# Sixteen of 43 contraction tiles of the down projection as 2x2 block products with seven multiplications

## The chip, the cores and the metric

The kernel runs on one core of a Trainium2 chip. A core has a tensor engine for matrix products (PE, with PEld its loads of the stationary operand), a vector engine (DVE), a scalar engine (ACT), GpSimd (POOL), and SyncE (SP), which here issues nearly all DMAs. Each engine takes its instructions in the order in which they stand in the program and waits at each until its operands are there. The metric is the device time of one execution in microseconds (us).

## The reference

The program is one decoder layer over 256 tokens of width 2048, all in float32: a norm, a mix of three branches with an output projection `w_o`, a second norm, a gated MLP, a final norm. The part that matters here is the end of it:

```python
h = rms_norm(x, norm2_g[l])
up = causal_dwconv(h @ ffn_up[l], ffn_conv_w[l])          # 2048 -> 2 x 5504
gt, vl = jnp.split(up, 2, axis=-1)
x = x + (jax.nn.silu(gt) * vl) @ ffn_down[l]              # 5504 -> 2048
...
return rms_norm(x, final_g)
```

The last product has 256 rows (tokens), a contraction of 5504 = 43 tiles of 128, and 2048 columns.

## The kernel before, in words

A float32 product is made of three passes in the type float32r: an operand is cut into an upper part and a lower rest, and the sum is hi\*hi + lo\*hi + hi\*lo. So each weight tile that arrives by DMA in a `raw` buffer (128x1024, 512 KB, 5 buffers) is **split**: ACT writes the upper part `wh` (line 75), DVE the rest `wl` (line 76). `wh` and `wl` have three buffers each, so that a split may run three chunks ahead of the products that use it.

**The up projection** (`gemm_t`) runs over 43 groups of 256 columns, four chunks each. Behind each group stands `up_group`: it folds the PSUM result, applies the three convolution taps and the gate, and splits the result into one tile of `fa` (lines 181 and 182). `fa` holds 43 tiles, [128 channels, upper parts of 256 tokens | rests of 256 tokens].

**The down projection** (`gemm_n`, called at lines 589 to 593) runs over four blocks of 512 columns. A chunk is two contraction tiles of 512 columns; it is split once, and then gives 2 tiles x 2 token halves x 3 passes = 12 matmuls of 128x512, eight with `wh` (lines 143 and 145) and then four with `wl` (line 150). Each block has a pair of PSUM banks of its own out of three, so the result of one block is taken up (`take`: the residual sum on DVE, its square sum on ACT, the product with the final gain) while the next one runs. `posts` is the list of such pieces of work; they are emitted behind the second chunk of the next block. For the last block the first 128 tokens are finished before the others, and `finish` scales and stores each half.

A scheduler sets the order of the instructions on each engine when the program is built, from the order in which they are emitted and its own estimate of times; `background` is a list of small pieces that `tick` emits one by one behind the newest split. The first chunks of the down projection are loaded by `first_weights` before the last `up_group` is emitted (line 555). The final pool `fin` is opened behind that.

Of the kernel before, what the change touches and what calls it, by code (L numbers as in the profile page):

```python
# [12 lines left out]
F32 = mybir.dt.float32  # L13
F32R = mybir.dt.float32r
# [16 lines left out]
# Columns of the packed per-channel parameters: [128, NV], a channel tile per column.  # L31
# [11 lines left out]
def hybrid_block(ctx: ExitStack, tc, xT, x, vec, w_in, pool_w, pool_p, conf_p, sconv_p, w_o, up, down, fg, out):  # L43
    """The activations lie transposed (channels on partitions, tokens free) up to w_o and from there
    to ffn_down. A float32 product is three passes of float32r: an operand a = ah + al exactly, ah
    its upper and al its lower 12 bits of mantissa, and the sum is ah*bh + al*bh + ah*bl."""
# [20 lines left out]
    def load_w(src, dst=None):  # L67
        """[128, kt, n] of a weight -> its upper and lower parts."""
# [59 lines left out]
    def gemm_n(src, act, nk, kt=2, ahead=(), last=None, finish=None):  # L128
# [3 lines left out]
        if last is None:  # L132
            ps = psg.tile([P, 2, 512], F32, name="g")
            out = [ps[:, t, :] for t in range(2)]
        else:
            out = [psm.tile([P, 512], F32, name="m") for t in range(2)]

        def products(ts, k0, wh, wl):
            n = wh.shape[1]
            for kk in range(n):  # L140
                k = k0 + kk
                for t in ts:
# [4 lines left out]
            for kk in range(n):  # L147
                k = k0 + kk
                for t in ts:
# [3 lines left out]
        nb = nk - (8 if last is not None else 0)  # L153
        for i, k0 in enumerate(range(0, nb, kt)):
            n = min(kt, nb - k0)
            products((0, 1), k0, *(ahead[i] if i < len(ahead) else load_w(src[:, k0:k0 + n, :])))
            if i == 1:
                run_posts()
        if last is not None:
            chunks = [(k0, load_w(src[:, k0:k0 + 2, :], [last[:, o + k0 - nb:o + k0 - nb + 2, :] for o in (0, 8)]))  # L160
                      for k0 in range(nb, nk, 2)]
            for t in range(2):
                for k0, w in chunks:
                    products((t,), k0, *w)
                finish(t, out[t])
# [474 lines left out]
```

## Time and profile before

| | us |
|---|---|
| median of three runs | 1506.58 (1506.28 to 1507.52) |
| span of the profiled execution, first to last instruction | 1504.9 |
| PE busy | 1488.4 (99% of the span) |
| DVE busy | 1079.8 (72%) |
| ACT busy | 765.7 (51%) |
| share of PE in the chain that ended last | 97% |

The run's time is 1.7 us longer than the span: that lies around the first and the last instruction. In the profile, matmuls are pipelined: the recorded 0.39 us of one 128x512 matmul is longer than the step from one to the next, so the step is read from rows that hold several. The views used below are the page, the chain of waits in order of time, groups of instructions by line and shape, the timeline of single engines, busy times by stretch with the granted clock, and the DMA issues.

### The profile page before, as it was taken

How to read it: one execution, taken by the hardware profiler on the slowest of the kernel's cores; microseconds unless marked ns; L12 is line 12 of the kernel's file. 1: busy time of each engine (PE TensorE's matmuls, PEld its weight loads, DVE VectorE, ACT ScalarE, POOL GpSimd, SP SyncE). 2: the span in 40 equal slices, each digit the busy share in tenths (PEclk: the TensorE clock that was granted, in tenths of full speed). 3: DMA queues.
4: the chain of work that ended last, by engine and by line, in shares of the span. 5: the costliest groups of instructions: out<-in, count | busy, mean ns of one | idle time of the engine just before them, and what ended most of it. 6: DMA issues, size and time to landing. Idle time of an engine off the chain costs nothing.

```text
span 1504.9 us, 21171 instructions
## 1 busy us (share of the span) xinstructions
PE 1488.4 (99%) x8090; PEld 1291.8 (86%) x8090; DVE 1079.8 (72%) x1450; ACT 765.7 (51%) x1019; POOL 23.8 (2%) x87
## 2 busy tenths in 40 slices
PE   7999999999999999999999999999999999999997
PEld 6888888888888888888888888888888888888886
DVE  5878888888888786666557777777777777455453
ACT  6544454454445565554555555555555555344343
POOL 0000000000000200000000000000000000000000
PEclk9999999999999999999999999999999999999999
DMA  8755555565555555557655555555555556666663
GB/s 276 242 190 186 181 181 191 190 199 189 193 186 188 188 183 188 190 186 248 183 181 190 188 190 186 191 188 187 189 188 190 189 188 212 197 197 195 189 196 119
DMA packets 81446, 290.08 MB, mean 193 GB/s; under 512 B 9152, under 2 KB 9664, under 8 KB 80960
## 3 DMA queue, kind: packets, MB, share of 16 engines
q1 hardware_dynamic: 80912, 287.94, 58.7%
q8 instruction: 63, 1.03, 0.3%
q10 hardware_dynamic: 432, 0.79, 0.1%
q14 instruction: 39, 0.32, 0.1%
HBM read 286.60 MB, written 2.10 MB: 192 GB/s over the span
## 4 chain that ended last, share of the span: by engine, by line
PE 97%; DMA 2%; issue 0%; ACT 0%; DVE 0%; DVEq 0%; POOLq 0%; POOL 0%; ACTq 0%
PE g L114 50%; PE g L118 26%; PE g L143 6%; PE g L150 6%; PE g L145 6%; PE m L150 1%; PE m L143 1%; PE m L145 1%; DMA raw<-in_w_in 1%; DMA raw<-in_x 0%; DMA raw<-in_xT 0%; PE m L510 0%; DMA g<-in_vec 0%; ACT wh L75 0%; DVE hT L251 0%
## 5 line engine op out<-in xcount | busy, mean ns | idle before, releaser
L76 DVE TENSOR_TENSOR wl<-raw,wh 128x1024 fp32r<-128x1024 f32 (+1 forms) x537 | 649.6, 1210 | 365.8 <-ACT wh L75 360.8
L75 ACT CAST wh<-raw 128x1024 fp32r<-128x1024 f32 (+1 forms) x537 | 556.1, 1036 | 634.6 <-PE g L114 238.3
L114 PE MATMUL g<-hT,wh 128*128 128x512 f32 x2912 | 733.9, 394 | 7.8 <-DVE hT L251 4.3
L114 PEld LDWEIGHTS g<-hT,wh 128*128 128x128 f32 x2912 | 524.7, 189 | 102.4 <-ACT wh L75 8.8
L118 PEld LDWEIGHTS g<-hT,wl 128*128 128x128 f32 x2912 | 399.1, 191 | 29.4
L118 PE MATMUL g<-hT,wl 128*128 128x256 f32 x2912 | 407.7, 283 | 0.0
L281 DVE SCALAR_TENSOR_TENSOR confwork<-confwork,vecs 128x256 f32<-128x256 f32 x240 | 107.8, 477 | 0.0
L145 PE MATMUL g<-wh,fa 128*128 128x512 f32 x258 | 100.4, 389 | 0.0
L143 PE MATMUL g<-wh,fa 128*128 128x512 f32 x258 | 100.4, 389 | 0.0
L546 DVE SCALAR_TENSOR_TENSOR cv<-sp,vecs,cv 128x256 f32<-128x256 f32 x172 | 71.7, 479 | 0.0
L150 PE MATMUL g<-wl,fa 128*128 128x512 f32 x258 | 69.2, 389 | 0.0
L171 ACT COPY fold_b<-g 128x512 f32<-128x512 f32 x115 | 66.9, 581 | 0.0
L145 PEld LDWEIGHTS g<-wh,fa 128*128 128x128 f32 x258 | 48.4, 188 | 10.1
L150 PEld LDWEIGHTS g<-wl,fa 128*128 128x128 f32 x258 | 48.4, 188 | 10.1
L143 PEld LDWEIGHTS g<-wh,fa 128*128 128x128 f32 x258 | 48.4, 188 | 10.0
L143 PE MATMUL g<-wh,merged 128*128 128x512 f32 x128 | 50.1, 391 | 0.0
L145 PE MATMUL g<-wh,merged 128*128 128x512 f32 x128 | 49.8, 389 | 0.0
L181 ACT CAST fa<-cv 128x256 fp32r<-128x256 f32 x43 | 17.5, 407 | 55.0 <-DVE cv L549 55.0
L174 DVE TENSOR_TENSOR fold_o<-g,fold_b 128x512 f32<-128x512 f32 x60 | 41.0, 683 | 0.0
L544 ACT ACTIVATE cv<-sp,vecs 128x256 f32<-128x256 f32 x86 | 39.0, 501 | 0.1
L150 PE MATMUL g<-wl,merged 128*128 128x512 f32 x128 | 34.2, 389 | 0.0
L182 DVE TENSOR_TENSOR fa<-cv,fa 128x256 fp32r<-128x256 f32 x43 | 18.3, 425 | 19.8 <-ACT fa L181 19.8
(131 smaller groups left out, 891.0 us busy)
## 6 DMA issues: line engine op xcount, KB each, us to landing
raw<-in_w_in SPq DMA_DIRECT2D x188, 512.0 KB, 3.6
raw<-in_up SPq DMA_DIRECT2D x172, 512.0 KB, 4.7
raw<-in_down SPq DMA_DIRECT2D x84, 512.0 KB, 3.8
raw<-in_w_o SPq DMA_DIRECT2D x32, 512.0 KB, 3.4
raw<-in_pool_p SPq DMA_DIRECT2D x16, 512.0 KB, 3.7
raw<-in_sconv_p SPq DMA_DIRECT2D x16, 512.0 KB, 4.8
raw<-in_conf_p SPq DMA_DIRECT2D x16, 512.0 KB, 3.6
raw<-in_x SPq DMA_DIRECT2D x4, 512.0 KB, 6.6
```

Source lines behind the costliest of these rows:

```text
L75: nc.scalar.copy(dst[0], raw)
L76: held["split"] = nc.vector.tensor_sub(dst[1], raw, dst[0].bitcast(F32)).ins
L114: nc.tensor.matmul(ps[:, j, :], lhsT=wh[:, kk, j * P:(j + 1) * P], rhs=act[:, k0 + kk, :], start=(k0 + kk == 0), stop=False)
L118: nc.tensor.matmul(ps[:, j, 0:S], lhsT=wl[:, kk, j * P:(j + 1) * P], rhs=act[:, k0 + kk, 0:S], start=False, stop=(k0 + kk == nk - 1))
L143: nc.tensor.matmul(out[t], lhsT=act[:, k, t * P:(t + 1) * P], rhs=wh[:, kk, :], start=(k == 0), stop=False)
L145: nc.tensor.matmul(out[t], lhsT=act[:, k, S + t * P:S + (t + 1) * P], rhs=wh[:, kk, :], start=False, stop=False)
L150: nc.tensor.matmul(out[t], lhsT=act[:, k, t * P:(t + 1) * P], rhs=wl[:, kk, :], start=False, stop=(k == nk - 1))
L171: nc.scalar.copy(b, ps[:, :, S:2 * S])
L174: nc.vector.tensor_add(out, ps[:, :, 0:S], b)
L281: nc.vector.scalar_tensor_tensor(acc[:, c, :], src, w, acc[:, c, :], op0=ALU.mult, op1=ALU.add)
L544: nc.scalar.activation(cv[:, h, :], sp[:, h, 0:S], AF.Copy, scale=V("ffn_w", c))
L546: nc.vector.scalar_tensor_tensor(cv[:, h, :], sp[:, h, q:q + S], V("ffn_w", c + q), cv[:, h, :], op0=ALU.mult, op1=ALU.add)
```

## The change

The contraction tiles 0 to 15 are taken in eight pairs (k, k+1). With the two token halves as rows, A is a 2x2 block matrix (a11, a21 from tile k, a12, a22 from tile k+1), and the weight's two tiles with two blocks of 512 columns give B. Winograd's form of Strassen's scheme makes the product with seven block multiplications and sums of blocks on both sides. The other 27 tiles stay plain, four block products each. A block product is three matmuls of 128x512, as before.

- The columns now run in two chunks `c` of 1024 (`chunk_pair`), each with four banks for the results ("11", "12", "21", "22") and four for the products p1, p5, p6, p7 that are added into several results: all eight banks of PSUM, the same ones for both chunks.
- `block_sums` makes the left sums once, for two pairs at a time (four calls, emitted one behind each of the first four plain tiles): a sum of the two parts of `fa`, four sums or differences of 128x2x128, and the splits of the results. s3 takes the place of a21 in `fa`.
- `pair` makes the right sums t1 to t4 per pair and chunk on DVE, four operations of 128x512, and splits four pieces where two plain tiles have two.
- `spread_products` adds p1, p5, p6, p7 to the residual `x1` after the last pair of a chunk, six operations on DVE. `take` and `finish` are now called per token half at the end of each chunk, directly and not through `posts`.
- The order of chunk 0 is nine plain tiles, then eight times a pair and two plain tiles, then two plain tiles; of chunk 1 it is eight times a pair and three plain tiles, then three. The last three tiles of each chunk are done for the first token half and then for the second.
- `first_weights` is no longer called for the down projection.

The diff, cut:

```diff
+SP = {i: 2 * i for i in range(0, 8, 2)}
+NS = 2 * len(SP)
...
-        ahead = first_weights(down[0])
         run_posts()
...
+    def block_sums(i):
+        def go():
+            r = fin.tile([P, 1024], F32, name="t", bufs=3)
+            v = fa[:, SP[i]:SP[i] + 4, :]
+            r = r.rearrange("p (k s) -> p k s", k=4)
+            nc.vector.tensor_add(r, v[:, :, 0:S].bitcast(F32), v[:, :, S:2 * S].bitcast(F32))
...
+            nc.vector.tensor_add(s1, a21, a22)
+            nc.vector.tensor_sub(s2, s1, a11)
+            nc.vector.tensor_sub(s4, a12, s2)
+            nc.vector.tensor_sub(s3, a11, a21)
+            o = sums[:, i:i + 2, :, :]
+            nc.scalar.copy(o[:, :, :, 0:P], q[:, :, 0:3, :])
+            nc.vector.tensor_sub(o[:, :, :, P:S], q[:, :, 0:3, :], o[:, :, :, 0:P].bitcast(F32))
+            d = v.rearrange("p (i e) s -> p i e s", e=2)[:, :, 0, :]
+            nc.scalar.copy(d[:, :, P:S], s3)
+            nc.vector.tensor_sub(d[:, :, S + P:2 * S], s3, d[:, :, P:S].bitcast(F32))
...
+    def product(name, left, right, first, last):
+
+        (ah, al), (bh, bl) = left, right
+        nc.tensor.matmul(bank[name], lhsT=ah, rhs=bh, start=first, stop=False)
+        nc.tensor.matmul(bank[name], lhsT=al, rhs=bh, start=False, stop=False)
+        nc.tensor.matmul(bank[name], lhsT=ah, rhs=bl, start=False, stop=last)
...
+            w11, = split_n(b11, 512)
+            nc.vector.tensor_sub(t1, b12, b11)
+            nc.vector.tensor_sub(t3, b22, b12)
+            put("p1", left_tile(k, 0), w11, last)
+            w1, w3 = split_n(t13, 1024)
+            nc.vector.tensor_sub(t2, b22, t1)
+            nc.vector.tensor_sub(t4, b21, t2)
+            put("p5", left_sum(i, 0), w1, last)
+            put("p7", left_tile(k, 1), w3, last)
+            w2, w4 = split_n(t24, 1024)
+            put("p6", left_sum(i, 1), w2, last)
+            w21, w22 = split_n(o, 1024)
+            put("21", left_tile(k + 1, 1), w4)
+            put("11", left_tile(k + 1, 0), w21)
+            put("12", left_sum(i, 2), w22)
...
+        for t in range(2):
+            for j, (k, _) in enumerate(tail):
+                plain(k, (t,), w[j], j == 2)
+            close(t)
...
             for t in range(2):
+                nc.vector.tensor_add(xs[:, t], bank["p1"].unsqueeze(1).broadcast_to([P, 2, 512]), xs[:, t])
+            nc.vector.tensor_add(xs[:, 0, 1], bank["p6"], xs[:, 0, 1])
+            for p in ("p6", "p7"):
+                nc.vector.tensor_add(xs[:, 1], bank[p].unsqueeze(1).broadcast_to([P, 2, 512]), xs[:, 1])
+            nc.vector.tensor_add(xs[:, :, 1], bank["p5"].unsqueeze(1).broadcast_to([P, 2, 512]), xs[:, :, 1])
...
+    def take(t):
+
+        for n in range(2):
+            residual(bank[f"{t + 1}{n + 1}"], x1[:, t, 512 * n:512 * n + 512], ss3[:, t, n:n + 1])
+        nc.vector.tensor_mul(x1[:, t, 0:1024], x1[:, t, 0:1024], fgb[:, 0:1024])
...
+    chunk_pair(0, first, take)
+    chunk_pair(1, second, finish)
```

How the change moves instructions is seen in their order on an engine. First DVE at the seam from the up to the down projection. Before, behind the last `up_group` (its last product of the gate, line 549, and its split into `fa`, line 182) there are only splits of down weights, one per chunk:

```order
L76 TENSOR_TENSOR wl_11859<-raw_11856,wh_11858 128x1024
L549 TENSOR_TENSOR cv_11776<-cv_11776 128x256
L182 TENSOR_TENSOR fa_7180<-cv_11776,fa_7180 128x256
L76 TENSOR_TENSOR wl_11877<-raw_11874,wh_11876 128x1024
L76 TENSOR_TENSOR wl_11895<-raw_11892,wh_11894 128x1024
L76 TENSOR_TENSOR wl_11913<-raw_11910,wh_11912 128x1024
```

Now the four `block_sums` stand there (line 562 the sum r, 567 to 570 the four sums, 573 and 576 the splits). From the first r to the split of the eighth plain tile, `wl_11962`, which may be called S7 (the tiles of chunk 0 counted from S0), there are 30 DVE instructions: 4 of r, 20 of 128x2x128, 3 of 128x6x128, and the splits of S5, S6 and S7. The last twelve rows of the stretch:

```order
L562 TENSOR_TENSOR t_11894<-fa_7180 128x1024
L569 TENSOR_TENSOR t_11867<-t_11865,t_11867 128x2x128
L576 TENSOR_TENSOR fa_7180<-t_11867,fa_7180 128x2x128
L567 TENSOR_TENSOR t_11896<-t_11894 128x2x128
L570 TENSOR_TENSOR t_11896<-t_11894 128x2x128
L573 TENSOR_TENSOR hT_11783<-t_11867,hT_11783 128x6x128
L568 TENSOR_TENSOR t_11896<-t_11896,t_11894 128x2x128
L576 TENSOR_TENSOR fa_7180<-t_11896,fa_7180 128x2x128
L569 TENSOR_TENSOR t_11896<-t_11894,t_11896 128x2x128
L586 TENSOR_TENSOR wl_11962<-raw_11959,wh_11961 128x1024
L573 TENSOR_TENSOR hT_11783<-t_11896,hT_11783 128x6x128
L586 TENSOR_TENSOR wl_11980<-raw_11977,wh_11979 128x1024
```

The splits of S7 and of S8 (`wl_11980`) have moved behind all 20 of these small operations. On PE, at S7, six matmuls with upper parts (`wh_11961` of S7 and `wh_12001` of the first pair's p1) stand ahead of the first one that needs `wl_11962`:

```order
L596 MATMUL g_11784<-wh_11961,fa_7180 128x512
L597 MATMUL g_11784<-wh_11961,fa_7180 128x512
L596 MATMUL g_11785<-wh_11961,fa_7180 128x512
L597 MATMUL g_11785<-wh_11961,fa_7180 128x512
L596 MATMUL m_11787<-wh_12001,fa_7180 128x512
L597 MATMUL m_11787<-wh_12001,fa_7180 128x512
L598 MATMUL g_11784<-wl_11962,fa_7180 128x512
```

Before, no matmul of a later chunk stood ahead of a chunk's own: a chunk was eight with `wh` and four with `wl`.

The second place is DVE where one block of columns ends and the next begins. Before, the taking up of block 0 (lines 496 and 570) stood behind two splits of block 1's weights:

```order
L76 TENSOR_TENSOR wl_12178<-raw_12175,wh_12177 128x1024
L76 TENSOR_TENSOR wl_12196<-raw_12193,wh_12195 128x1024
L496 TENSOR_TENSOR x1_6534<-g_11795,x1_6534 128x512 x2
L76 TENSOR_TENSOR wl_12219<-raw_12216,wh_12218 128x1024
L570 TENSOR_TENSOR x1_6534<-x1_6534,fgb_11793 128x2x512
L76 TENSOR_TENSOR wl_12237<-raw_12234,wh_12236 128x1024
```

Now, between chunk 0 and chunk 1 (lines 483 and 680 are `take`; g_11784 holds banks 11 and 12, g_11785 banks 21 and 22; 630, 631, 634, 635 make t1, t3, t2, t4; `t_12816` is the t1 of the pair after; `wl_12727` is the split of t1 and t3 for p5 and p7, `wl_12739` that of t2 and t4 for p6 and 21):

```order
L483 TENSOR_TENSOR x1_6534<-g_11784,x1_6534 128x512 x2
L631 TENSOR_TENSOR t_12715<-raw_12713,raw_12711 128x512
L483 TENSOR_TENSOR x1_6534<-g_11785,x1_6534 128x512
L680 TENSOR_TENSOR x1_6534<-x1_6534,fgb_11781 128x1024
L483 TENSOR_TENSOR x1_6534<-g_11785,x1_6534 128x512
L586 TENSOR_TENSOR wl_12727<-t_12715,wh_12726 128x1024
L680 TENSOR_TENSOR x1_6534<-x1_6534,fgb_11781 128x1024
L634 TENSOR_TENSOR t_12716<-raw_12713,t_12715 128x512
L630 TENSOR_TENSOR t_12816<-raw_12812 128x512
L635 TENSOR_TENSOR t_12716<-raw_12713,t_12716 128x512
L586 TENSOR_TENSOR wl_12739<-t_12716,wh_12738 128x1024
L586 TENSOR_TENSOR wl_12746<-raw_12713,wh_12745 128x1024
```

The adds of chunk 0's last banks and both products with the gain now stand ahead of the splits that chunk 1's first pair needs.

## Rows read from the trace of the kernel before

**Rows 1.** The page: span; busy time, share, instructions; granted clock by slice, in tenths.
```profile
span 1504.9 us, 21171 instructions
PE 1488.4 (99%) x8090; PEld 1291.8 (86%) x8090; DVE 1079.8 (72%) x1450; ACT 765.7 (51%) x1019; POOL 23.8 (2%) x87
PEclk9999999999999999999999999999999999999999
```
**Rows 2.** The chain that ended last, at the seam: start us, us, what.
```profile
1261.30 0.95 PE g L118 x8
1272.25 0.91 PE g L150 x4
1274.97 0.91 PE g L150 x4
```
**Rows 3.** Groups by shape, 1225 to 1505 us: busy us, mean ns; idle before, releasers.
```profile
L76 DVE TENSOR_TENSOR wl<-raw,wh 128x1024 fp32r<-128x1024 f32 x91 | 111.4, 1225 | 109.4 <-ACT wh L75 109.4
L75 ACT CAST wh<-raw 128x1024 fp32r<-128x1024 f32 x91 | 95.8, 1053 | 129.6 <-PE g L145 92.9 <-PE m L145 20.4 <-issue 12.7
L496 DVE TENSOR_TENSOR x<-g,x 128x512 f32<-128x512 f32 x6 | 3.9, 686 | 0.0
L570 DVE TENSOR_TENSOR x<-x,fgb 128x1024 f32<-128x1024 f32 x3 | 3.7, 1217 | 0.0
L76 DVE TENSOR_TENSOR wl<-raw,wh 128x512 fp32r<-128x512 f32 x4 | 2.8, 692 | 4.4 <-PE g L150 4.1 <-issue 0.2
L182 DVE TENSOR_TENSOR fa<-cv,fa 128x256 fp32r<-128x256 f32 x5 | 2.1, 425 | 2.4 <-ACT fa L181 2.4
L181 ACT CAST fa<-cv 128x256 fp32r<-128x256 f32 x5 | 2.0, 407 | 6.5 <-DVE cv L549 6.5
```
**Rows 4.** DVE in order of time at the seam: start us, us, instruction [idle before].
```profile
1266.40 1.67 DVE L546 SCALAR_TENSOR_TENSOR cv<-sp,vecs,cv 128x256 f32<-128x256 f32 x4
1267.98 1.22 DVE L76 TENSOR_TENSOR wl<-raw,wh 128x1024 fp32r<-128x1024 f32 x1
1269.12 0.42 DVE L549 TENSOR_TENSOR cv<-cv 128x256 f32<-128x256 f32 x1
1270.01 0.42 DVE L182 TENSOR_TENSOR fa<-cv,fa 128x256 fp32r<-128x256 f32 x1 [0.47 <-ACT fa L181]
1273.42 1.23 DVE L76 TENSOR_TENSOR wl<-raw,wh 128x1024 fp32r<-128x1024 f32 x1 [1.23 <-ACT wh L75]
```
**Rows 5.** Stretches: PE, PEld, DVE, ACT, POOL busy (x instructions), PEclk, DMA, GB/s.
```profile
1300.00:1350.00 50.00, 50.00 (x222) 41.42 (x221) 24.94 (x22) 20.64 (x24) 0.00 (x0) 1.00 0.63 194
1497.00:1498.00 1.00, 0.00 (x0) 0.00 (x0) 0.21 (x1) 0.68 (x2) 0.00 (x0) 1.00 0.34 123
1498.00:1499.00 1.00, 0.00 (x0) 0.00 (x0) 0.41 (x1) 0.41 (x1) 0.55 (x1) 0.61 0.00 0
1499.00:1500.00 1.00, 0.00 (x0) 0.00 (x0) 0.87 (x2) 0.53 (x1) 0.00 (x0) 0.50 0.00 0
```
**Rows 6.** DMA issues, 1262 to 1496 us: KB each, median us to landing.
```profile
raw<-in_down SPq DMA_DIRECT2D x77, 512.0 KB, 4.1
```
**Rows 7.** The end, in order of time: start us, us, engine, instruction [idle before].
```profile
1495.58 0.61 PE L150 MATMUL m<-hT,fa 128*128 128x512 f32 x2
1496.23 0.69 DVE L496 TENSOR_TENSOR x<-m,x 128x512 f32<-128x512 f32 x1 [1.80 <-PE m L150]
1496.96 0.63 ACT L497 ACTIVATE scratch<-x 128x512 f32<-128x512 f32 x1 [2.87 <-DVE x L496]
1497.71 0.21 DVE L580 TENSOR_SCALAR r<-ss,part 128x1 f32<-128x1 f32 x1 [0.79 <-ACT scratch L497]
1498.59 0.62 DVE L584 TENSOR_SCALAR x<-x,r 128x768 f32<-128x768 f32 x1 [0.67 <-POOL r L581]
1499.13 0.75 DVE L586 SCALAR_TENSOR_TENSOR x<-x,r,fgb 128x512 f32<-128x512 f32 x1
1499.90 0.33 SPq L587 DMA_DIRECT2D out<-x  x1
```

More of the change, by code (lines that the diff above doesn't have):

```diff
@@ L148, in products @@
                 k = k0 + kk
-                for t in ts:
+                for t in range(2):
                     nc.tensor.matmul(out[t], lhsT=act[:, k, t * P:(t + 1) * P], rhs=wl[:, kk, :],
                                      start=False, stop=(k == nk - 1))
[L153 to L156, printed above, removed]
             if i == 1:
                 run_posts()
[L159 to L165, printed above, removed]
         return out
@@ new lines, in chunk_pair, with put, plain, pair @@
+    def chunk_pair(c, order, close):
+        seen = set()
+        live = {"11": 0, "12": 0, "21": 0, "22": 0}
+        pairs_left = [sum(1 for _, i in order if i >= 0)]
+        def put(name, left, right, last=False):
+            product(name, left, right, name not in seen, last)
+            seen.add(name)
+        def plain(k, ts, w, last=False):
+            for t in ts:
+                for n in range(2):
+                    put(f"{t + 1}{n + 1}", left_tile(k, t), w[n], last)
+        def pair(k, i):
+            e, o = (load_raw(down[c][:, k + j:k + j + 1, :])[0][:, 0, :] for j in range(2))
+            last = pairs_left[0] == 1
+            b11, b12 = halves(e)
+            b21, b22 = halves(o)
+            t13, t24 = (fin.tile([P, 1024], F32, name="t", bufs=3) for _ in range(2))
+            (t1, t3), (t2, t4) = halves(t13), halves(t24)
+            w11, = split_n(b11, 512)
[13 more added lines that the diff above has]
+            put("12", left_sum(i, 2), w22)
+            pairs_left[0] -= 1
+            if last:
+                posts.append(spread_products(c))
+        tail = order[-3:]
+        for k, i in order[:-3]:
+            if i >= 0:
+                pair(k, i)
+            else:
+                plain(k, (0, 1), split_n(load_raw(down[c][:, k:k + 1, :])[0][:, 0, :], 1024))
+                run_posts()
+                tick(1)
+        assert all(i < 0 for _, i in tail)
+        w = [split_n(load_raw(down[c][:, k:k + 1, :])[0][:, 0, :], 1024) for k, _ in tail]
+        for t in range(2):
+            for j, (k, _) in enumerate(tail):
+                plain(k, (t,), w[j], j == 2)
+            close(t)
@@ L589, in hybrid_block @@
-    for n in range(3):
-        posts.append(take(n, gemm_n(down[n], fa, KF, ahead=ahead)))
-        ahead = ()
-    room = hp.tile([P, 16, 512], F32R, name="hT")
-    gemm_n(down[3], fa, KF, last=room, finish=finish)
+        nc.scalar.activation(x1[:, t, 0:1024], x1[:, t, 0:1024], AF.Copy, scale=r)
+        nc.scalar.dma_start(ov[:, t, 0:1024], x1[:, t, 0:1024])
+        for n in range(2):
+            o = 1024 + 512 * n
+            nc.vector.scalar_tensor_tensor(x1[:, t, o:o + 512], x1[:, t, o:o + 512], r, fgb[:, o:o + 512], op0=ALU.mult, op1=ALU.mult)
+            nc.sync.dma_start(ov[:, t, o:o + 512], x1[:, t, o:o + 512])
@@ new lines, in hybrid_block @@
+    single = [(k, -1) for k in range(KF) if not any(p <= k < p + 4 for p in SP.values())]
+    paired = [(SP[i] + 2 * j, i + j) for i in SP for j in range(2)]
+    for i in SP:
+        background.append(block_sums(i))
+    first, second = list(single[:9]), []
+    for n, p in enumerate(paired):
+        first += [p, *single[9 + 2 * n:11 + 2 * n]]
+        second += [p, *single[3 * n:3 * n + 3]]
+    first += single[9 + 2 * len(paired):]
+    second += single[3 * len(paired):]
+    chunk_pair(0, first, take)
```

62 lines of the change are left out of this document (36 added, 26 removed).

## Prediction, made before the changed kernel ran

> **What bounds the kernel now.** I read the page first: PE is busy 99% of the span [rows 1]. The chain of waits then tells whether busy is also necessary: from the last up matmuls on it holds nothing but PE, and two groups of four matmuls that close successive chunks start 2.72 us apart [rows 2]. So 12 matmuls of 128x512 cost 2.72 us, 0.227 us each, without a gap. The stretch in the middle of the down projection shows what lies beside that: DVE busy 24.9 of 50 us, ACT 20.6 [rows 5]. The groups by shape show that DVE's idle time ends on ACT's cast and ACT's on PE [rows 3]: weights are split as soon as PE frees a buffer, not when DVE finds time. Matmuls removed are time removed, as long as every split still comes before its matmul. That is the question, since the change puts its additions on DVE, which has half its time free on average but works in order. Hence I go through DVE's order at each place where much is added.
>
> DVE prices [rows 3]: 1.225 us for 128x1024, 0.69 for 128x512, 0.425 for 128x256, also with an operand in PSUM (0.686). Behind a 1.22 us split the next instruction starts after 1.14 [rows 4], so I count steps: 1.14, 0.61 and 0.34, or the full duration plus 0.04 where an operation needs the one just ahead of it. The 128x6x128 splits lie between rows 256 and 1024: 0.96 us, step 0.87. The 128x2x128 operations have no row of their own; I give them the step of 256 elements. No less is to be had; strided operands and waits could make it 0.46.
>
> **Removed.** Eight pairs in two chunks spare one block product each: 16 x 3 = 48 matmuls of 1032, 48 x 0.227 = **10.9 us**. Bytes loaded stay the same.
>
> **The seam, S0 to S8.** The last up matmuls end at 1261.30 + 0.95 = 1262.25 [rows 2]. `first_weights` is gone, but the scheduler put the first casts and loads ahead of the last `up_group` anyway, so nothing is lost there; the load of the final gain and the allocation of `fin` come behind the loads of S0 to S8. The split into `fa` ended at 1270.43 [rows 4]. A chunk's `wh` is now free after its 11th matmul instead of its 8th, 0.68 us later, so I put this at 1271.2. From there DVE has, to the end of S7's split: four r and the splits of S5, S6, S7, 7 x 1.14 = 8.0; 20 small ones, 20 x 0.34 = 6.8; three of 128x6x128, 2.6; and about 0.1 of waiting for ACT. Sum 17.5, so `wl_11962` is there at 1288.7. S5 (1273.6) and S6 (1278.6) come in time. PE reaches S7 at 1262.25 + 7 x 2.72 = 1281.3, has six matmuls that need no `wl_11962` (1.36), and stands still from 1282.7: **6.1 us** lost. With small operations at 0.46 it is 8.5; I keep 5.5 to 9.
>
> S8's split follows at 1290.7, just in time. Behind it DVE makes w11's split, t1 to t4 and the split for p5 and p7 in a row: 1.21 + 0.61 + 0.61 + 0.73 + 0.73 + 1.23 from there to 1295.0, while PE, through S8 at 1293.4, wants that split at 1294.1. With the p6 split 0.35 late too, the first pair loses **1.3 us** (0 to 2).
>
> **Steady pairs.** A pair and two plain tiles take PE 45 x 0.227 = 10.2 us; DVE 5 x 0.61 + 5 x 1.14 and some dependent steps, 9.0; ACT five casts at 1.05 and one of half the size, 5.9. It holds, but with little to spare at one point: the split for p6 stands behind t1 of the pair after, which waits for that pair's raw tile. This load is issued when a plain tile's split, 3.7 us before the pair starts, frees its buffer; at 4.1 us to landing [rows 6] t1 is done about 1.0 us into the pair, the split at 2.2, and PE wants it at 2.5. I cost it at nothing; should landing take a microsecond more, 0.7 us per pair, 5 us for seven. Chunk 1 has three plain tiles per pair and more room.
>
> **End of each chunk.** The six adds of `spread_products`, 5 x 1.14 + 0.61 = 6.3 us of DVE, stand among the splits of the last pair and of the tail. The first waits for the last p1 and delays the split behind it; the scheduler gave PE upper-part matmuls to fill in. Counting DVE from 0.9 us (p1 done and seen) over eight steps of 1.14 and 0.61, the first tail tile's split ends at 9.6, and PE, with 0.2 lost before, is at 8.6 when it needs it: **1.2 us**, in both chunks 2.4 (1 to 4).
>
> **Between the chunks.** Let E be the end of the last matmul's step in chunk 0. The adds of banks 11 and 12 occupy DVE until about E - 0.2, since PE's order finishes these banks only seven matmuls before E; then t3 (E + 0.4), the add of 21 (E + 1.05), the product with the gain (2.2), the add of 22 (2.8), and only then the split for p5 and p7, at E + 4.0. PE has done p1 and four upper-part matmuls and waits. Then come the second product with the gain (5.1), t2, the next t1, t4 (7.0), ACT's cast of t2 and t4 (8.1), DVE's split (9.4): PE finishes p6 at E + 9.65, where 12 matmuls without a wait would be at 2.72. **6.9 us** lost (5 to 9). Before, two splits stood ahead of this work and the next block had banks of its own; now PE has no work without these splits.
>
> **The end.** Before, the last add started 0.2 us after E and the last DMA was issued at E + 3.87 (E = 1495.58 + 2 x 0.227 = 1496.03) [rows 7]. Now the first token half's scaling, two of 0.75 us, fills DVE until E + 0.7, as its banks close only 18 matmuls (4.1 us) before E; then two adds (2.0), squares and their sums (2.75), one reduction more than before (0.25) and the 0.9 us from sums to scaling as in rows 7 (3.9), two scalings (5.3), the DMA. **1.45 us** more (0.5 to 2).
>
> **The clock.** With PE idle from 1496.2, the granted clock read 1.00 in 1497 to 1498, 0.61 in the next microsecond and 0.50, which is 1.2 GHz, from 1499 on [rows 5]. PE's waits of 6.1 us at S7 and 3.5 us ahead of p6 are idle stretches of that kind, so I expect the lower level behind them. No row here shows matmuls at 1.2 GHz. From nothing, if the clock returns at once, to about 2.7 us per chunk of 12 for as long as it stays: I take 0.3 us at the seam (the wait of the first pair absorbs most) and 1.7 at the boundary, **2.0 us** (0 to 8). The Trainium skill asks to leave no idle gaps between bursts of matmuls, or the array goes back to the slow clock (TensorE: Matmul & The Clock Gate, "Why this matters for your kernels"); the trace agrees as far as the fall goes, with 0.50 after the last matmul, and without that rule this term would be nothing and the sum below 7.25.
>
> **Sum.** -10.9 + 6.1 + 1.3 + 2.4 + 6.9 + 1.45 + 2.0 = +9.25 us: span 1504.9 + 9.25 = 1514.2, and with the 1.7 us that lie between span and median, **1516 us**. By the terms' ends, it is -10.9 + 5.5 + 0 + 1 + 5 + 0.5 + 0 = +1.1 to -10.9 + 9 + 2 + 5 + 4 + 9 + 2 + 8 = +28; not all go one way.
>
> **Rivals.**
> - *The sums are done in time.* The stall at S7 is the difference of two long walks; if DVE needs 11.4 us instead of 17.5 up to S7, PE does not wait there. For it: DVE is idle 25 of 50 us. Against: that idle time lies behind casts, and the stretch has 30 instructions, nearly all without a wait between. Then 1516 - 6.1 - 1.3 - 0.3 = 1508.3, not slower by the bound used here. Decided where S7's split ends before 1283. 0.13.
> - *The waits between the chunks overlap too*, as DVE's queue lets splits through that I place behind the adds: without either place, -10.9 + 2.4 + 1.45 = -7, 1499.5. The order of the program speaks against it, half a microsecond here or there is all I see. 0.07.
> - *The clock stays low.* If PE runs at half rate over the rest of S7, S8 and the first pair (41 matmuls, 9.3 us more, of which waits absorb 1.3) and half as long at the boundary, 1516 - 2 + 8 + 4 = 1526. For it: PE's busy share is low for 9 us at the boundary. Against: the clock stands at its highest digit in all 40 slices, the first with PE's early waits too [rows 1]. The rule named above would work this way too, as a mechanism of this kernel. 0.08.
> - *Loads bind in chunk 0's pairs*: 5 us, 1521. For it: the small room at the next raw tile; against: 4.1 us is a median under nearly the same load. 0.10.
>
> That leaves 0.62 for the forecast, itself spread over 1511 to 1521. What a measurement of this kernel tells from no change is 0.2%, 3 us: 1503.6 to 1509.6. Faster 0.08, the same 0.15 (the first rival and the low edge of the forecast), slower 0.77. Range 1507 to 1522: two in ten are left out, the second rival and the long clock.
>
> **What would show it.** PE's waits: one of about 6 us for DVE (line 598) near 1283 us, one or two of 1 us in the first pair and ahead of each tail, about 7 us in pieces in p5 to p6 of chunk 1's first pair, each ended by DVE's split (line 586) or ACT's cast behind it. PE's matmuls 48 fewer; granted clock below 1.00 behind the two long waits; DVE without idle time from 1271 to 1296. Wrong it is if PE runs through S7, if the splits at the boundary come before the products with the gain, or if the pairs in between lose time.

## The result and the profile after

The changed kernel takes 1524.5 us (median of four runs, 1522.3 to 1526.1), the kernel before 1507.1 on the same chip: ratio 1.0113, 95% interval 1.0100 to 1.0126. The direction was forecast, the size not: 17 us instead of 9, and 2.5 us above the range. The profiled execution is the quickest of the four; all accounts below are of its span, against [rows 1].

```profile
span 1520.4 us, 21302 instructions
PE 1487.8 (98%) x8042; PEld 1284.7 (84%) x8042; DVE 1170.8 (77%) x1583; ACT 795.6 (52%) x1057; POOL 23.8 (2%) x87
PEclk9999999999999999999999999999999999999999
```

The 48 matmuls are gone (8090 to 8042), yet PE is busy as long as before (1487.8 for 1488.4 us), and the clock line is all nines again: a slice of 38 us hides what happens in five. To see it, take the starts of successive matmuls of the down projection and count, for every step that is clearly longer than the rest, what it has beyond 0.227 us. The sum is 25.0 us, where 48 x 0.227 = 10.9 were saved. Behind the last matmul's step lie 10.3 us instead of 8.9 (1520.4 - 1510.1; before 1504.9 - 1496.0). So -10.9 + 25.0 + 1.4 = +15.5, which is the whole difference of the spans (1520.4 - 1504.9). Two small terms are left out and cancel: the down projection starts 0.6 us earlier than before (1261.5 for 1262.1), and its many other steps are together 0.6 us longer.

PE's waits from 1225 to 1525 us follow (engine, line, releaser: us in total, times, longest). Lines 596, 597 and 598 are the three matmuls of a block product, hi\*hi, lo\*hi and hi\*lo in the order left\*right; only 598 needs the rest `wl` of the weight. Lines 585 and 586 are ACT's cast and DVE's split of a weight or of a right sum.

```profile
PE g L598 <- DVE wl L586: 10.1, 9, 5.9
PE g L596 <- ACT wh L585: 3.3, 1, 3.3
PE m L598 <- DVE wl L586: 1.0, 1, 1.0
PE m L596 <- ACT wh L585: 1.0, 1, 1.0
```

**The seam.** PE in order of time (start, duration, instruction [idle before]):

```profile
1281.67 0.40 PE L597 MATMUL m<-wh,fa 128*128 128x512 f32 x1
1287.93 0.79 PE L598 MATMUL g<-wl,fa 128*128 128x512 f32 x1 [5.86 <-DVE wl L586]
1288.52 0.63 PE L596 MATMUL g<-wh,fa 128*128 128x512 f32 x1
1288.95 0.63 PE L597 MATMUL g<-wh,fa 128*128 128x512 f32 x1
...
1293.70 0.39 PE L596 MATMUL g<-wh,fa 128*128 128x512 f32 x1
1293.93 0.40 PE L597 MATMUL g<-wh,fa 128*128 128x512 f32 x1
```

DVE over the end of that wait:

```profile
1286.32 0.42 DVE L569 TENSOR_TENSOR t<-t 128x256 f32<-128x256 f32 x1
1286.66 1.22 DVE L586 TENSOR_TENSOR wl<-raw,wh 128x1024 fp32r<-128x1024 f32 x1
1287.79 0.95 DVE L573 TENSOR_TENSOR hT<-t,hT 128x768 fp32r<-128x768 f32 x1
```

S7's split (1286.66) ends at 1287.9, between small operations in steps of 0.34 us, as counted. Behind the wait the matmuls start 0.43 us apart instead of 0.23, until 1293.2. The view by stretches (columns as in [rows 5]) has the reason:

```profile
1288.20:1293.30 5.10, 5.10 (x13) 3.93 (x14) 5.07 (x8) 1.24 (x2) 0.00 (x0) 0.50 0.73 206
1384.00:1396.00 12.00, 6.64 (x22) 4.06 (x21) 10.48 (x14) 6.67 (x12) 0.00 (x0) 0.84 0.27 85
1396.00:1440.00 44.00, 43.49 (x184) 35.09 (x184) 32.84 (x36) 22.29 (x23) 0.00 (x0) 0.96 0.56 185
```

PE is busy all 5.1 us at a granted clock of 0.50, 1.2 GHz: this is the price that [rows 5] could not show. The twelve long steps cost 2.6 us here, those behind the waits between the chunks 2.8.

**The pairs.** DVE in chunk 0's second pair:

```profile
1303.22 1.23 DVE L586 TENSOR_TENSOR wl<-t,wh 128x1024 fp32r<-128x1024 f32 x1 [0.58 <-ACT wh L585]
1306.36 0.69 DVE L630 TENSOR_TENSOR t<-raw 128x512 f32<-128x512 f32 x1 [1.91 <-DMA raw<-in_down]
1306.97 1.22 DVE L586 TENSOR_TENSOR wl<-t,wh 128x1024 fp32r<-128x1024 f32 x1
```

The matmul that waited for it:

```profile
1307.10 0.39 PE L597 MATMUL g<-wh,hT 128*128 128x512 f32 x1
1308.24 0.50 PE L598 MATMUL g<-wl,hT 128*128 128x512 f32 x1 [0.75 <-DVE wl L586]
```

L630 is t1 of the *next* pair; it waits 1.9 us for that pair's raw tile, and the current pair's split for p6 stands behind it. In the trace this tile's load was issued at 1300.7, 4.1 us before the pair starts on PE (1304.8), and took 5.6 us to land. DVE's waits by releaser, 1300 to 1380 and then 1400 to 1490 us, show that this repeats in both chunks:

```profile
DVE t L630 <- DMA raw<-in_down: 7.9, 6, 1.9
...
DVE t L630 <- DMA raw<-in_down: 7.1, 6, 1.7
```

PE passes on 2.6 us of it in chunk 0 and 2.5 in chunk 1. From issue to landing a tile takes 4.8 us (median, 1300 to 1385 us), 4.1 before [rows 6], and the loads come in bursts with nothing between. DMA's busy share in tenths and its GB/s, 1300 to 1345 us in 40 slices, and below them the busy share of the kernel before in the same stretch:

```profile
DMA  9899610007999871003799993002799896001899
GB/s 335 299 331 339 259 51 11 0 0 153 375 360 346 291 280 80 0 0 47 259 364 317 364 379 131 4 0 40 244 302 324 342 339 280 0 0 25 127 320 404
```

```profile
DMA  7644284683837776185494958774757747376474
```

**Between the chunks** DVE works through what was listed, and PE loses 6.0 us in three pieces (at 1387.7, 1389.9 and 1393.9):

```profile
1386.86 1.22 DVE L680 TENSOR_TENSOR x<-x,fgb 128x1024 f32<-128x1024 f32 x1
1387.99 0.68 DVE L483 TENSOR_TENSOR x<-g,x 128x512 f32<-128x512 f32 x1
1388.59 1.22 DVE L586 TENSOR_TENSOR wl<-t,wh 128x1024 fp32r<-128x1024 f32 x1
1389.72 1.22 DVE L680 TENSOR_TENSOR x<-x,fgb 128x1024 f32<-128x1024 f32 x1
1390.86 0.69 DVE L634 TENSOR_TENSOR t<-raw,t 128x512 f32<-128x512 f32 x1
1391.46 0.68 DVE L630 TENSOR_TENSOR t<-raw 128x512 f32<-128x512 f32 x1
1392.07 0.69 DVE L635 TENSOR_TENSOR t<-raw,t 128x512 f32<-128x512 f32 x1
1393.92 1.23 DVE L586 TENSOR_TENSOR wl<-t,wh 128x1024 fp32r<-128x1024 f32 x1 [1.17 <-ACT wh L585]
```

**The end** answers to [rows 7]: the first half's scaling holds up the second half's adds.

```profile
1509.49 1.42 DVE L694 SCALAR_TENSOR_TENSOR x<-x,r,fgb 128x512 f32<-128x512 f32 x2 [0.66 <-POOL r L689]
1510.82 1.28 DVE L483 TENSOR_TENSOR x<-g,x 128x512 f32<-128x512 f32 x2
```

### The profile page after: what moved, and what is told of

Its sections match the earlier page's. It is cut to its first block, busy times and chain, and to the rows that moved or that the text cites. A ratio compares the mean times of both kernels' runs of the same rounds, so it can differ in the third digit from the quotient of the medians.

```text
span 1520.4 us, 21302 instructions
## 1 busy us (share of the span) xinstructions
PE 1487.8 (98%) x8042; PEld 1284.7 (84%) x8042; DVE 1170.8 (77%) x1583; ACT 795.6 (52%) x1057; POOL 23.8 (2%) x87
## 4 chain that ended last, share of the span: by engine, by line
PE 90%; DVE 4%; DMA 3%; issue 1%; ACT 1%; DVEq 0%; POOLq 0%; POOL 0%; ACTq 0%
PE g L117 49%; PE g L121 25%; PE g L598 3%; PE g L596 3%; PE g L597 3%; DVE wl L586 2%; PE g L142 2%; PE g L144 2%; PE g L149 2%; DMA raw<-in_down 2%; DMA raw<-in_w_in 1%; ACT wh L585 1%; DMA raw<-in_x 0%; PE m L598 0%; DMA raw<-in_xT 0%
## 5 line engine op out<-in xcount | busy, mean ns | idle before, releaser
L79 DVE TENSOR_TENSOR wl<-raw,wh 128x1024 fp32r<-128x1024 f32 (+2 forms) x453 | 549.1, 1213 | 257.0 <-ACT wh L78 256.4
L78 ACT CAST wh<-raw 128x1024 fp32r<-128x1024 f32 (+2 forms) x453 | 469.2, 1036 | 508.7 <-PE g L117 237.8
L598 PE MATMUL g<-wl,fa 128*128 128x512 f32 x264 | 104.3, 398 | 7.3 <-DVE wl L586 7.3
L585 ACT CAST wh<-raw 128x1024 fp32r<-128x1024 f32 (+1 forms) x86 | 83.3, 971 | 50.8 <-PE g L597 42.9
L596 PE MATMUL g<-wh,fa 128*128 128x512 f32 x264 | 104.3, 395 | 0.0
L597 PE MATMUL g<-wh,fa 128*128 128x512 f32 x264 | 103.9, 394 | 0.0
L586 DVE TENSOR_TENSOR wl<-raw,wh 128x1024 fp32r<-128x1024 f32 (+1 forms) x86 | 93.3, 1120 | 5.4 <-ACT wh L585 4.6
L585 ACT CAST wh<-t 128x1024 fp32r<-128x1024 f32 x32 | 33.6, 1052 | 61.1 <-PE g L597 44.5
L597 PEld LDWEIGHTS g<-wh,fa 128*128 128x128 f32 x264 | 50.4, 191 | 10.8
L596 PEld LDWEIGHTS g<-wh,fa 128*128 128x128 f32 x264 | 50.4, 191 | 10.1
L586 DVE TENSOR_TENSOR wl<-t,wh 128x1024 fp32r<-128x1024 f32 x32 | 39.1, 1222 | 17.7 <-ACT wh L585 17.3
L168 ACT CAST fa<-cv 128x256 fp32r<-128x256 f32 x43 | 17.5, 407 | 55.1 <-DVE cv L536 55.1
```

The costliest lines, as they stand in the source:

```text
L78: nc.scalar.copy(dst[0], raw)
L79: held["split"] = nc.vector.tensor_sub(dst[1], raw, dst[0].bitcast(F32)).ins
L585: nc.scalar.copy(h, src)
L586: held["split"] = nc.vector.tensor_sub(l, src, h.bitcast(F32)).ins
L596: nc.tensor.matmul(bank[name], lhsT=ah, rhs=bh, start=first, stop=False)
L597: nc.tensor.matmul(bank[name], lhsT=al, rhs=bh, start=False, stop=False)
```

## The experiments

"Lost" is what PE's steps in the down projection have beyond 0.227 us, from each run's trace; beside it how it divides: up to 1300 us (the stall at S7 and the clock behind it), the boundary with the clock behind it, and the rest (pairs, adds, small steps). In pace_only the early part belongs to a pair. The columns are of one profiled execution each; with the change at the end they give the differences of the medians only to about 2 us.

| kernel | us (median) | ratio, 95% interval | lost | seam | boundary | rest |
|---|---|---|---|---|---|---|
| changed | 1524.5 | 1.0100 to 1.0126 | 25.0 | 8.6 | 8.8 | 7.6 |
| t_late | 1517.1 | 1.0049 to 1.0079 | 17.6 | 7.7 | 7.4 | 2.5 |
| plain_first | 1516.8 | 1.0046 to 1.0080 | 17.4 | 7.6 | 1.6 | 8.2 |
| paced | 1507.3 | 0.9994 to 1.0012 | 9.6 | 0 | 2.8 | 6.8 |
| order_only | 1525.9 | 1.0113 to 1.0144 | 26.9 | 9.3 | 4.5 | 13.1 |
| order_late | 1519.5 | 1.0064 to 1.0095 | 21.6 | 9.0 | 8.0 | 4.6 |
| pace_only | 1521.7 | 1.0081 to 1.0109 | 21.1 | 0 | 8.4 | 12.7 |
| raw6 | 1519.8 | 1.0070 to 1.0097 | 22.1 | 8.4 | 7.3 | 6.4 |
| nopairs | 1509.3 | 1.0005 to 1.0023 | 0.5 | 0 | 0.5 | 0 |
| best3 | 1505.6 | 0.9981 to 1.0000 | 6.4 | 0 | 1.8 | 4.6 |
| best5 | 1511.5 | 1.0018 to 1.0041 | 13.3 | 3.9 | 4.3 | 5.1 |
| best8 | 1506.0 | 0.9982 to 1.0000 | 7.6 | 0 | 1.7 | 5.9 |
| best9 | 1503.6 | 0.9967 to 0.9986 | 5.7 | 0 | 0.7 | 5.0 |

**t_late.** Theory: t1 and t3 make the waits in the pairs. They are held behind their own pair's first split:

```diff
-            nc.vector.tensor_sub(t1, b12, b11)
-            nc.vector.tensor_sub(t3, b22, b12)
+            with tc.issue_after(held["split"]):
+                nc.vector.tensor_sub(t1, b12, b11)
+                nc.vector.tensor_sub(t3, b22, b12)
```

> The changed kernel, with t1 and t3 of a pair placed behind the pair's own first split instead of ahead of the pair before's p6 split; the same operations. Theory A (three separate delays in DVE's order; in the pairs DVE stands before a raw tile that has not landed, while the next split is ready): PE's waits in the pairs, 5.1 us with their follow-up, go, and the time falls from 1524.5 to about 1519.5 (1518 to 1521.5); the stall at S7 (6.0) and the waits between the chunks (6.0) stay. Rival B (DVE simply has too much work in the down projection, so what one place gains another pays): 1523 or more. Rival C (the loads themselves are too slow): the wait moves to the pair's first split, 1523 or more.

It gains 7.4 us, and the traces agree: the 5.1 of the pairs, 1 at the seam, 1.4 at the boundary. The waits themselves give 5.6 of this (5.1 in the pairs, 0.5 at the boundary); the other 1.8 are fewer steps at the low clock, behind a stall at S7 as long as in the changed kernel (6.0) and behind the boundary's waits, and why they are fewer no run isolates. Of DVE's waits from 1300 to 1380 us none for a load is left (L670 is the first add of `spread_products`):

```profile
DVE wl L586 <- ACT wh L585: 7.9, 6, 1.3
DVE x L670 <- PE m L598: 1.1, 1, 1.1
```

The loads still take 4.5 us (median, 1300 to 1385 us). So it was the place of t1 in DVE's order, not the loads as such.

**plain_first.** Chunk 1 begins with two plain tiles, so that the boundary's adds do not stand ahead of a pair's splits:

```diff
-    first, second = list(single[:9]), []
+    first, second, left = list(single[:9]), list(single[:2]), single[2:]
...
-        second += [p, *single[3 * n:3 * n + 3]]
+        second += [p, *left[3 * n:3 * n + 3]]
...
-    second += single[3 * len(paired):]
+    second += left[3 * len(paired):]
```

> The changed kernel, with two plain tiles ahead of the first pair in chunk 1, so that PE has work while DVE takes up chunk 0. Theory A: of the 6.0 us of waits between the chunks and the 2.9 us at the low clock behind them about 2 remain; 1524.5 - 7 = 1517.5 (1515.5 to 1520). Rival D (what binds there are the PSUM banks, which chunk 1 shares with chunk 0, and not the splits): the plain tiles need banks 11 to 22 at once and wait for the adds, 1522 or more. Rival B: 1522 or more.

As expected: 7.7 us gained, the boundary's waits down to 0.8 + 0.3, the stall at the seam untouched (6.0).

**paced.** The block sums one behind every fourth plain tile, and 15 plain tiles first so that they are all done when the first pair comes:

```diff
-        background.append(block_sums(i))
+        background.extend([block_sums(i), *pause(3)])
...
-    first, second = list(single[:9]), []
+    first, second = list(single[:15]), []
...
-        first += [p, *single[9 + 2 * n:11 + 2 * n]]
+        first += [p, single[15 + n]]
...
-    first += single[9 + 2 * len(paired):]
+    first += single[15 + len(paired):]
```

> The changed kernel, with the four block_sums four plain tiles apart instead of one behind the other; chunk 0 is then 15 plain tiles, eight times a pair and one plain tile, four plain tiles. The same work on every engine. Theory A: the stall of 6.0 us at S7 and the 2.5 us at the low clock behind it go, and pairs with one plain tile between cost 1 to 2 us more; 1524.5 - 7 = 1517.5 (1515.5 to 1520). Rival B (amount, not order): chunk 0 keeps its length, the wait moves into the pairs, 1522 or more.

The stall at the seam goes, as expected, but the time falls by 17 us instead of 7. The three next runs look for the other ten.

**order_only** (paced's tile order, the sums in a row), **order_late** (the same with t_late's edit) and **pace_only** (the sums apart, the changed kernel's tile order):

> Chunk 0 in the order of `paced` (15 plain tiles, eight times a pair and one plain tile, four plain tiles), but the four block_sums one behind the other as in the changed kernel. `paced` fell by 17 us where 7 were expected, so its two edits are taken apart. Theory A (the sums in a row cost the stall at S7 and the low clock behind it, 6.0 + 2.5; the other 8.5 of `paced` came from the order of tiles: its boundary waits are 2.4 instead of 6.0, since the scheduler placed the next pair's splits ahead of the adds): 1507.3 + 8.5 = 1515.8 (1514 to 1517.5), with a wait of 6 us at S7 and about 2.4 between the chunks. Rival E (the order of tiles did nearly all, a stall at S7 is made up later by splits that are then ahead): 1510 or less.

> The tile order of order_only (15 plain tiles, eight times a pair and one plain, four plain), the four block sums still in a row, and t1 and t3 held behind their own pair's first split, as in t_late. In order_only's trace every pair of chunk 0 has t3 (L631) of the next pair ahead of the split of p2/p4 of the current one on VectorE, and it waits 0.9 to 1.5 us each time for a tile of raw; in paced, which has the same tile order, it stands behind the next pair's own first split and never waits. Theory A (the place of t3 on VectorE makes the waits): the waits of order_only's pairs, about 8 us in the two chunks, go; the stall at the seam (6.5) and the clock behind it (2.5) stay: 1525.9 - 8 = 1518, range 1516 to 1520. Rival B (the loads are late by themselves in this tile order, and the sums apart cure them by another way): the waits only move to the split behind: 1523 or more.

> The changed kernel with its own tile order, and three empty pieces between the block sums, so that the four sums stand four plain tiles apart; nothing else. Theory A (the stall at the seam and the low clock behind it come from the sums standing in a row; everything else is a matter of tile order and of the place of t1 and t3): 6.0 + 2.5 go, and the pairs' waits (about 5), the boundary (6 + 2.9) and the adds stay: 1524.5 - 8.5 = 1516, range 1514 to 1518. Rival B (what paced gained over the sum of its parts came from the sums apart): 1509 or less. Rival C (sums between the pairs delay the pairs): above 1519.

order_only misses by ten: the new tile order alone gains nothing. DVE over one of its pairs:

```profile
1329.38 0.69 DVE L630 TENSOR_TENSOR t<-raw 128x512 f32<-128x512 f32 x1
1331.04 0.69 DVE L631 TENSOR_TENSOR t<-raw 128x512 f32<-128x512 f32 x1 [0.98 <-DMA raw<-in_down]
1331.65 1.22 DVE L586 TENSOR_TENSOR wl<-t,wh 128x1024 fp32r<-128x1024 f32 x1
1332.78 2.96 DVE L586 TENSOR_TENSOR wl<-raw,wh 128x1024 fp32r<-128x1024 f32 x3
```

The same stretch of paced:

```profile
1327.87 2.95 DVE L586 TENSOR_TENSOR wl<-raw,wh 128x1024 fp32r<-128x1024 f32 x3
1330.74 0.69 DVE L631 TENSOR_TENSOR t<-raw 128x512 f32<-128x512 f32 x1
1331.34 0.69 DVE L634 TENSOR_TENSOR t<-raw,t 128x512 f32<-128x512 f32 x1
1332.06 0.69 DVE L635 TENSOR_TENSOR t<-raw,t 128x512 f32<-128x512 f32 x1
1332.67 1.22 DVE L586 TENSOR_TENSOR wl<-t,wh 128x1024 fp32r<-128x1024 f32 x1
```

With the sums in a row the scheduler puts the next pair's t3 (L631) ahead of this pair's split, and it waits 9.0 us over eight pairs; in paced it stands behind the next pair's own splits, where its tile has long been there. order_late holds it there by hand, and t1 with it, so that t3's share alone is not measured: 6.4 us back, within its range, none of DVE's waits for a load left. And pace_only shows the other side: the seam's 8.6 us go, but the third sum now runs right ahead of the first pair (from 1284.0) and the fourth among the pairs (from 1307.2), PE waits 1.7 + 0.4 + 1.2 and 0.7 + 0.4 + 1.2 us behind them, and the rest grows by 5.1; only 2.8 us are gained, as the third rival said. So paced combined three things: sums apart, all of them before the first pair needs DVE, and by chance t3 in its place. Why its boundary is cheap too (2.8 us, 8.0 in order_late) I didn't isolate; the place of chunk 1's first t3 is again the scheduler's choice.

**raw6.** A sixth raw buffer, in the space of one t buffer, as the other way to have the tile in time:

```diff
-        raw = wp.tile([P, 1024], F32, name="raw", bufs=5)
+        raw = wp.tile([P, 1024], F32, name="raw", bufs=6)
```

(and `bufs=3` of t to 2)

> The changed kernel with six raw buffers instead of five, paid for by two buffers t instead of three. Theory A (a pair's first raw tile comes late because the ring of five frees its buffer late): t1's wait for the load goes from 15 us of DVE in the down projection to under 4, PE's waits in the pairs fall by 3 to 5 us, 1520.5 (1518.5 to 1522.5). Rival C (the loads are slow by themselves): 1523 or more, t1 waits as long as before.

4.7 us gained, within the range, but not where they were expected. From 1290 to 1490 us L630's waits for loads are 0.9 us where they were 15.0 (7.9 + 7.1), and L631 has 4.4 of its own, so the waits moved in part from t1 to t3: PE still loses 3.9 us in the pairs where it lost 5.1, 1.2 less and not 3 to 5. The boundary gives 1.5, and 1.8 of the gain lie outside what PE's steps show, no more than executions differ before the down projection. A tile that comes earlier helps less than taking t1 and t3 out of the way of the split (t_late).

**nopairs.** The new structure (1024-wide chunks, four banks, both halves' tails) with all 43 tiles plain, 1032 matmuls:

```diff
-SP = {i: 2 * i for i in range(0, 8, 2)}
-NS = 2 * len(SP)
+SP = {}
+NS = 2
```

> The changed kernel with no pairs: all 43 tiles plain in two chunks of 1024 columns, no sums, no products to spread; 1032 matmuls as before. It leaves the structure alone: shared banks, take and finish per token half. Theory A: nothing is in DVE's way, so between the chunks under 1 us, the end 1 us longer than before: 1508.5 (1507.5 to 1510). Rival D (banks shared by both chunks bind): 1511 or more. If the structure itself were a gain, below 1506.5.

1509.3, within the range: the structure costs 2.2 us by itself, so that as it stands 8.7 of the 10.9 are left to be had. Its end is 1.5 us longer than before (10.3 us behind the last step), and part of that can be taken back, as best8 shows.

**The way to a faster kernel.** best3 is the diffs of paced, plain_first and t_late together. best5 has t_late's, the sums three tiles apart and 13 plain tiles first, two plain tiles first in chunk 1 and then two behind each pair, the last three tiles bank by bank, and the product with the gain on GpSimd:

```diff
-    first, second = list(single[:9]), []
+    first, second = list(single[:13]), list(single[:2])
...
-            for j, (k, _) in enumerate(tail):
-                plain(k, (t,), w[j], j == 2)
+            for n in range(2):
+                for j, (k, _) in enumerate(tail):
+                    put(f"{t + 1}{n + 1}", left_tile(k, t), w[j][n], j == 2)
...
-        nc.vector.tensor_mul(x1[:, t, 0:1024], x1[:, t, 0:1024], fgb[:, 0:1024])
+        nc.gpsimd.tensor_mul(x1[:, t, 0:1024], x1[:, t, 0:1024], fgb[:, 0:1024])
```

> All three: block_sums paced, chunk 1 with two plain tiles first, t1 and t3 behind their pair's first split. Theory A: the gains add, -7 - 7 - 5 = -19, 1505.5 (1502 to 1509), which is about the 10.9 us of matmuls removed less the adds of the four products (2.4), the longer end (0.9) and 3 to 6 us of remaining waits against 1507 before. Rival B: 1513 or more, since DVE's work is the same.

> best3 with a new order (chunk 0: 13 plain tiles, eight times a pair and one plain tile, six plain; chunk 1: two plain, eight times a pair and two plain, nine plain), so that the adds of the four products have more plain tiles to lie beside; block_sums three tiles apart; the tail by banks, so that 11 and 21 close before 12 and 22; the product with the gain on GpSimd. Theory A: of best3's 6.4 us of PE waits the two of 0.9 at the tails and about 1 at the boundary go, the end is 0.7 shorter: 1505.6 - 3.5 = 1502 (1500.5 to 1504). Rival B (DVE is full in the pairs when fewer plain tiles lie between): 1505 or more.

best3 comes as forecast. best5 is 9.5 us off: the sums three tiles apart leave 2.1 us of stall at the seam and the low clock behind it, and the boundary loses 2.0 and 1.6. There GpSimd's product runs:

```profile
1386.59 2.94 POOL L682 TENSOR_TENSOR x<-x,fgb 128x1024 f32<-128x1024 f32 x1 [3.33 <-ACT scratch L484]
```

and DVE beside it:

```profile
1387.19 2.88 DVE L631 TENSOR_TENSOR t<-raw 128x512 f32<-128x512 f32 x1
1390.00 0.68 DVE L632 TENSOR_TENSOR t<-raw 128x512 f32<-128x512 f32 x1
```

This product runs until 1389.5; the DVE operation that started beside it, 0.68 us elsewhere, ends at 1390.1.

best8 goes back to best3, with two plain tiles behind each pair of chunk 1 in place of three and the others at its end, and changes how the chunks end; `spread_products` now gives a list of its adds, one for each plain tile that follows:

```diff
-                posts.append(spread_products(c))
+                background.extend(spread_products(c))
...
+            for n in range(2):
+                for j, (k, _) in enumerate(tail):
+                    put(f"{t + 1}{n + 1}", left_tile(k, t), w[j][n], j == 2)
+                close(t, n)
...
+        elif t == 1 and n == 1:
+            with tc.issue_after(held["res"]):
+                apply(0)
+            scale(1)
+            apply(1)
```

best9 corrects best8 by its trace:

```diff
-    bank = {"11": gA[:, 0, :], "12": gA[:, 1, :], "21": gB[:, 0, :], "22": gB[:, 1, :], ...
+    bank = {"11": gA[:, 0, :], "21": gA[:, 1, :], "12": gB[:, 0, :], "22": gB[:, 1, :], ...
...
-                background.extend(spread_products(c))
+                if c:
+                    background.extend(spread_products(c))
+                else:
+                    posts.append(lambda: [f() for f in spread_products(c)])
```

(and plain tiles through the banks in the order 11, 21, 12, 22)

> best3 (15 plain tiles first, sums apart, t1 and t3 held behind their own first split, two plain tiles ahead of chunk 1's first pair) with three edits of the end: chunk 1 has two plain tiles behind each pair and nine at its end, the adds of the products are given out one behind each plain tile, and the last three tiles are taken bank by bank, so that a finished bank is added while TensorE is on the next, with the second half's add ahead of the first half's scaling. From best3's trace: of the adds' two waits of 0.9 us chunk 1's goes, and of the 11.4 us behind the last matmul about 1.5 go: 1505.6 - 2.4 = 1503.2, range 1502 to 1506 (before: 1507). If the adds and the tail are hidden or replaced by other waits, it stays at 1505.6. Above 1507 the three edits would have opened a new wait.

> best8 with its three new waits taken out. From best8's trace: chunk 0's adds, given out before its last three tiles, cost TensorE 0.77 + 1.29 + 0.57 us, where the run of adds behind the last pair cost 0.9 in best3; so chunk 0 has them in a row again. TensorE waited 0.95 us in the last tile, since the second half's bank 22 lies in one PSUM tile with bank 21, which VectorE was just reading; so the halves' banks are paired as (11, 21) and (12, 22), and a plain tile runs through the banks in the order 11, 21, 12, 22. At the boundary 1.06 + 0.29. Expected: 1506.0 - 1.7 - 0.95 = 1503.4, with part of the boundary's 1.3 to be had by the new pairing of the banks: range 1501.5 to 1505.5; ratio to before about 0.9975. If what TensorE no longer waits for is made up elsewhere (VectorE at 98 % in the pairs of chunk 0), it stays at 1505 to 1506.

best8 shortens the end (9.5 us behind the last step, 11.2 in best3) and pays for it twice: 2.6 us at chunk 0's adds, and 0.95 in the last tile, where PE waits for an add that reads another bank of the same PSUM tile:

```profile
1492.51 0.50 PE L596 MATMUL g<-wh,fa 128*128 128x512 f32 x1 [0.79 <-DVE x L686]
```

best9 takes 1503.6 us, 0.9976 of the kernel before (0.9967 to 0.9986): 3.6 us faster than before and 21 faster than the change as it was made. The sum came as forecast, its parts did not: the wait in the last tile is gone and the boundary is down by 1.1, but chunk 0's adds still cost 2.1 us (0.9 was expected). PE's waits in its down projection:

```profile
PE g L598 <- DVE wl L586: 1.0, 2, 0.6
PE g L596 <- DVE x L483: 0.5, 1, 0.5
PE g L596 <- ACT wh L585: 0.2, 1, 0.2
```

The stretch of three of chunk 0's pairs:

```profile
1336.50:1360.00 23.50, 23.44 (x101) 18.36 (x100) 23.28 (x28) 13.61 (x16) 0.00 (x0) 1.00 0.61 200
```

DVE is busy 23.28 of 23.50 us there: a pair and one plain tile take it 7.8 us where PE needs 33 x 0.227 = 7.5, so DVE is now what bounds these pairs.

## Why the prediction fell short

Right, with the profiled execution's numbers beside the terms:

- *Removed*: 10.9, and 48 matmuls fewer.
- *The stall at S7*: 6.0 for 6.1; the split at 1287.9 for 1288.7. PE stood still 0.8 us earlier too (1281.9 for 1282.7; 0.6 of it is this execution's earlier start), so the two offsets cancel; DVE's walk from the first r to the end of this split took 17.4 us for 17.5. The walk through DVE's order held, the rival "the sums are done in time" did not.
- *End of each chunk*: 2.4 for 2.4. *The end*: 1.4 for 1.45.
- *Between the chunks*: 6.0 for 6.9, in order and cause.

Wrong:

- ***Steady pairs*, the step that failed**: "I cost it at nothing; should landing take a microsecond more, 0.7 us per pair". Landing took 4.8 us instead of 4.1, and 5.6 and 5.5 for the tiles behind PE's first two waits in the pairs (at 1308.2 and 1319.0 us); PE lost 5.1 us in the pairs, and taking the cause away gave back 7.4 in all, 5.6 of them in waits (t_late). The mechanism had been named and priced at 5 us in a rival with 0.10, but for chunk 0 alone, which lost 2.6; that its 5 meets the 5.1 of both chunks is luck. I chose zero because the median of the rows of before just sufficed. Those rows are of a kernel whose loads are spread out (its DMA row above has no empty slice); here the raw buffers come free in bursts, and the loads with them. And "Chunk 1 has ... more room" was no step of the argument but a guess: there a pair and three plain tiles go once round the five raw buffers, so the next pair's first tile takes the buffer that the present pair has only just freed, and DVE's waits are about as long (7.1 for 7.9 us).
- ***The clock***, mis-sized: 5.4 us for 2.0, 2.6 at the seam and 2.8 at the boundary. At the seam I had 0.3 for it, beside a wait of 1.3 in the first pair. The low clock made PE later than that pair's splits (the one for p5 and p7 ends at 1294.2, PE takes its lower part at 1295.8), so the pair's own wait became 0; together they cost 2.6 us, not 1.6. The walk of that wait was also added up wrongly: 1.21 + 0.61 + 0.61 + 0.73 + 0.73 + 1.23 is 5.1 us, not the 4.3 from 1290.7 to 1295.0. The trace has 4.3, since w11's split is half a tile and takes a step of 0.6. The Trainium skill's rule on idle gaps (TensorE: Matmul & The Clock Gate, "Why this matters for your kernels") was right in kind; the trace gives its price here, steps of 0.43 us for 0.23.

By terms: +5.1 (pairs) + 3.4 (clock) - 1.3 (first pair) - 0.9 (boundary) - 0.1 (S7) = +6.2, and the span was 1520.4 where 1514.2 was forecast. The other 2.3 us are the median's distance from the profiled execution's span, 4.1 us where the kernel before has 1.7: the other three executions were 1.6 to 3.8 us longer than the profiled one. Executions differ by as much before anything that was changed: in the 14 profiles the 500th matmul starts between 98.0 and 101.8 us (99.0 in this one, 99.7 in the kernel before), and from there to the first matmul of the down projection all take 1162.4 us. Whether the three longer executions lost their time there, no profile shows; it stays open.

## What to carry to other kernels

On an engine that works in order, an operation's cost is also what stands behind it: before counting busy time, ask of each operation that can wait for a DMA which later work is queued behind it, and put it behind the work that is due first. Where the margin of a load is under a microsecond, give it the price of the next longer landing, not zero. And a stall of several microseconds can cost PE more than its length: behind the stall of 6 us or a little more at the seam the low clock took from 1.5 us (plain_first) to 2.8 (order_only) on top.

## What the runs showed of the hardware

- Behind waits of 5.9 and 3.3 us PE ran at a granted clock of 0.50, its matmuls 0.43 us apart, for about 5 us although it waited no more than 0.3 us in them, and then at full speed. Behind shorter waits it fell in some places and not in others: it fell behind one of 2.1 us (best5, seam: 0.50 from 1285.0 to 1288.2 us) and three that sum to 2.5 (order_only, boundary: 0.52 from 1400.2 to 1403.6), and stayed at 1.00 behind 2.0 (best5, boundary), 1.7 + 0.4 + 1.2 (pace_only) and 2.3 (plain_first, a pair). So no length of wait that decides it comes out of these runs.
- A DVE operation that starts while GpSimd's product of 128x1024 runs ends only after it (best5): L631 took 2.88 us instead of 0.68, and a split 2.64 instead of 1.22 (1381.7 to 1384.3, the product from 1380.9 to 1383.3). The Trainium skill says that the two engines share a pair of ports, which whichever of them starts first holds for its whole instruction while the other is blocked, also where DVE reads two inputs from SBUF and GpSimd reads SBUF (SBUF — State Buffer, "SBUF: two separate sides"); these two rows agree.
